# A hybrid encoder block: where tiles lie modulo 256 bytes, and which engine scales the first half of each mid norm

## The chip, the core and the metric

The kernel runs on one core of a Trainium2 chip. It computes in float32, its large products as fp32r, and is one launch. The metric is the device time of that launch in microseconds. TensorE (PE in the profile) multiplies; VectorE (DVE), ScalarE (ACT) and GpSimd (POOL) do the rest; SyncE (SP) issues every DMA. A tile in SBUF has 128 partitions, and where it lies is given by its first byte within a partition.

## The reference

One layer of a bidirectional encoder on 1024 tokens of width 1024. Each sub-layer is normed before and after, and added to the residual:

```python
h = _rms_norm(x, g_mix_pre[l])
proj = h @ w_in[l]
...
mix = jnp.concatenate([attn_o, dn_o], axis=-1) @ w_out[l]
x = x + _rms_norm(mix, g_mix_post[l])
c = _memory_cross_attention(_rms_norm(x, g_cross_pre[l]), _rms_norm(mem, g_mem[l]),
                            w_cq[l], w_ckv[l], w_co[l])
x = x + _rms_norm(c, g_cross_post[l])
f = _swiglu(_rms_norm(x, g_ffn_pre[l]), w_gate_up[l], w_down[l])
x = x + _rms_norm(f, g_ffn_post[l])
```

attn_o is a windowed attention, dn_o a gated delta rule that is scanned in both directions, and the cross attention reads 256 memory tokens.

## The kernel before

**Products.** Every float32 operand of a large product is split into two fp32r parts, hi (a rounding on ScalarE, L102) and lo (the rest, on VectorE or GpSimd, L103, or L106 with a scale). A product is three matmuls: hi by hi, hi by lo, lo by hi. `load_w` fetches a block of weights (`wraw`) and makes `whi` and `wlo` of it, two blocks in flight.

**Stages, in order of time.** The input projections with the convolutions and chunk preparations of the delta rule (matmuls `pg` on L261; `wabr` on L315 is a short extra projection); the scans (`psc`) between windows of attention and the memory's keys and values (`pck`, `pcv`); `mid_gemm` for the output projection (`pmg`, L1016), once for each half of the tokens; the cross attention (`pcq`, `pcs`, `pco`); `mid_gemm` again; the gate and up projections in seven products of sums and differences of quarters (`pA`, `pB`, `pD`, `pE`, L1191); the down projection (`pdA`, `pdD`, `pdX`, L1381 and L1474). A scheduler orders the instructions of each engine; `ORDER_1` to `ORDER_3` set the order in which the early parts are issued to it.

**A mid norm.** After its eight blocks of weights, `mid_gemm` does for each of four tiles of 128 tokens: GpSimd makes the first rstd (L1028, L1029), VectorE scales z and adds the residual (L1030), ScalarE squares z and sums it (L1033), GpSimd makes the second rstd from that (L161, L162), and ScalarE scales z by it into `xr` (L1036). `turn_norm` or `turned_k` then turns `xr` on TensorE. A call with `hf` 0 is the first half of the tokens, and its turning comes while the second half's product already runs.

**Rows of the profile.** A matmul reads out<-streamed operand, weights: in `pA<-s,whi` the activations `s` stream past the weights `whi`; in `pmg<-whi,b` the weights' block streams past the activations `b`. Names are tags: `b` is any tile of opB (activations at the left), `s` the first operand of opA (at the right), `x` the one of opC, `s0h` to `s3l` sums of weights.

**Where tiles lie.** Pools grow from both ends of the SBUF. The left end holds `cst` first (ident 512 bytes, mhalf 64, phalf 64, cols 512, from byte 16512), then `wp` (the weights' blocks) and most others; the right end holds `off` (a tile of 32 bytes, which only takes room) and then those pools that are opened with `side="right"`. In the built program, modulo 256:

| tiles | end | before | after |
|---|---|---|---|
| wraw, whi, wlo, opB (b), opC (x), opB3, dhl, t4h, t4l, bhi, blo, ph, vhl, qs, khi, kr, vr, mT, U | left | 0 | 192 |
| cph, cpl | left | 128 | 192 |
| hhi, hlo, opA (s), s0h to s3l, sr, pz, kv of the scan, S, mraw, gt | right | 192 | 192 |
| wabr, xt, z and xr of the second mid_gemm | right | 64 | 64 |
| z and xr of the first mid_gemm | left | 0 | 192 |
| ident (what turns a tile) | left | 128 | 128 |

Of the kernel before, what the change touches and what calls it, by code (L numbers as in the profile page):

```python
# [10 lines left out]
F32 = mybir.dt.float32  # L11
F32R = mybir.dt.float32r
I32 = mybir.dt.int32
AF = mybir.ActivationFunctionType
ALU = mybir.AluOpType
# [4 lines left out]
P = 128  # L20
# [55 lines left out]
def tile_hybrid_block(  # L76
# [6 lines left out]
    nc = tc.nc  # L83
# [24 lines left out]
    def pool(name, bufs, **kw):  # L108
        return tc.tile_pool(name=name, bufs=bufs, reuse_waits="tile", **kw)

    cst = ctx.enter_context(pool("cst", 1))
# [6 lines left out]
    def load_w(src, k, n, eng=None, after=None):  # L118

        with tc.high_priority(AHEAD):  # L120
            raw = wp.tile([P, k, n], F32, tag="wraw", name="wraw")
            with ExitStack() as order_:
                if after:
                    order_.enter_context(tc.issue_after(after.ins))
                nc.sync.dma_start(raw, src.rearrange("(k p) n -> p k n", p=P))
            hi = wp.tile([P, k, n], F32R, tag="whi", name="whi")
            lo = wp.tile([P, k, n], F32R, tag="wlo", name="wlo")
            split(hi, lo, raw, eng=eng)
        return hi, lo
# [2 lines left out]
    ident = cst.tile([P, P], F32, name="ident")  # L132
    mhalf = cst.tile([P, 16], F32, name="mhalf")
    nc.gpsimd.memset(mhalf, -0.5)
    phalf = cst.tile([P, 16], F32, name="phalf")
    nc.gpsimd.memset(phalf, 0.5)
    cols = cst.tile([P, P], F32, name="cols")
    p12 = ExitStack()
# [19 lines left out]
    def rstd_of(rs, ss, n, eps):  # L158

        w = ss.shape[-1]  # L160
        nc.gpsimd.tensor_scalar(rs, ss, n, eps, ALU.mult, ALU.add)  # L161
        nc.gpsimd.tensor_tensor(rs, rs, mhalf[:, :w], ALU.pow)  # L162
# [836 lines left out]
    def mid_gemm(tz, act, w, gp, res, dst, hf, between=None):  # L999


        zs = [tz.tile([P, D], F32, tag="z", name="z", bufs=4) for _ in range(4)]
        sss = [tz.tile([P, 2], F32, tag="zss", name="zss", bufs=8) for _ in range(4)]
        for ch in range(2):
            cs = slice(ch * 512, (ch + 1) * 512)
            if ch and between:
                between()
            pp = [pg.tile([P, 512], F32, tag="pg", name="pmg") for _ in range(4)]
            for kp in range(4):
                whi, wlo = load_w(w[kp * 256:(kp + 1) * 256, cs], 2, 512)  # L1010
                for t in range(4):
                    tt = slice(t * P, (t + 1) * P)
                    for kk in range(2):
                        k = 2 * kp + kk
                        for i, (w_, a) in enumerate(((whi, 0), (whi, 1), (wlo, 0))):
                            nc.tensor.matmul(pp[t], act[a][:, k, tt], w_[:, kk, :], start=(k == 0 and i == 0),  # L1016
                                             stop=(k == KT - 1 and i == 2))
            for t in range(4):
                nc.scalar.activation(zs[t][:, cs], pp[t], AF.Square, accum_out=sss[t][:, ch:ch + 1])
                nc.vector.tensor_tensor(zs[t][:, cs], pp[t], gp[:, cs], ALU.mult)  # L1020
        xn = []
        for t in range(4):
            tok = slice(hf * HALF + t * P, hf * HALF + (t + 1) * P)
            z = zs[t]
            xr = tz.tile([P, D], F32, tag="xr", name="xr", bufs=XR)
            nc.sync.dma_start(xr, res[tok, :])
            rs = tz.tile([P, 1], F32, tag="prs", name="prs", bufs=4)
            nc.gpsimd.tensor_scalar(rs, sss[t][:, 1:2], sss[t][:, 0:1], D * EPS, ALU.add, ALU.add)  # L1028
            nc.gpsimd.tensor_tensor(rs, rs, mhalf[:, 0:1], ALU.pow)  # L1029
            nc.vector.scalar_tensor_tensor(z, z, rs, xr, ALU.mult, ALU.add)  # L1030
            nc.sync.dma_start(dst[tok, :], z)
            s2 = tz.tile([P, 1], F32, tag="ps2", name="ps2", bufs=4)
            nc.scalar.activation(xr, z, AF.Square, accum_out=s2)  # L1033
            r2 = tz.tile([P, 1], F32, tag="pr2", name="pr2", bufs=4)
            rstd_of(r2, s2, 1.0 / D, EPS)
            nc.scalar.activation(xr, z, AF.Identity, scale=r2)  # L1036
            xn.append(xr)
        return xn

# [11 lines left out]
    for hf in range(2):  # L1051
        for kp in range(4):
# [4 lines left out]
            split(mxT[hf][0][:, k2, :], mxT[hf][1][:, k2, :], raw[:, k2, :])  # L1057
    LR.close()
    xn0 = mid_gemm(tz, mxT[0], w_out, gp, x, d_x1, 0)
    h2T = [[opB.tile([P, KT, HALF], F32R, tag=b1, name=b1), opB_first[2]]]  # L1060
    xn1 = mid_gemm(tz, mxT[1], w_out, gp, x, d_x1, 1, between=lambda: turn_norm(xn0, "cross", *h2T[0], pin=True))
    h2T.append(operand(opA, "s0"))
    turn_norm(xn1, "cross", *h2T[1])
# [8 lines left out]

    L2 = ExitStack()
    tx = L2.enter_context(pool("tx", 2))

    def cross_q(hf):
        q = operand(opB, ("s1", "s2")[hf])
        for ct in range(KT):
            whi, wlo = load_w(w_cq[:, ct * P:(ct + 1) * P], KT, P, nc.gpsimd)
            pp = [pg.tile([P, 512], F32, tag="pg", name="pcq")]  # L1080
            gemm_b(whi, wlo, h2T[hf:hf + 1], pp)
            split(q[0][:, ct, :], q[1][:, ct, :], pp[0])
        return q
# [60 lines left out]
    def blocks(t):  # L1144
        return t[:, 0:HK], t[:, HK:KT]

    xn = mid_gemm(tz, q0, w_co, gp, d_x1, d_x2, 0)
    x1h, x1l = operand(opA, "s0")
    X11, X21 = (x1h[:, 0:HK], x1l[:, 0:HK]), (x1h[:, HK:KT], x1l[:, HK:KT])
# [252 lines left out]
    def residual(t, after=None):  # L1402
        xr = tp_.tile([P, D], F32, tag="xrf", name="xrf")
        with tc.issue_after((after or late).ins):
            nc.sync.dma_start(xr, d_x2[t * P:(t + 1) * P, :])
        return xr
# [57 lines left out]
    for t in range(4):  # L1464
# [14 lines left out]
        xr = residual(r)  # L1479
# [40 lines left out]
```

## Time and profile before

| | before |
|---|---|
| median of 3 runs | 1562.68 us (1558.62 to 1563.87) |
| the profiled execution, its own time | 1562.86 us |
| its span | 1561.1 us |
| mean granted TensorE clock | 0.99 |
| HBM read, written | 173.65 MB, 69.50 MB |
| matmuls, weight loads | 7451, 7451 |

Busy time of an engine is a union of its instructions; a matmul's recorded length overlaps its successor's, so the distance of two starts, not the length, tells how fast TensorE goes. Idle time behind a group of instructions is put down to what ended it. The lines themselves stand where they are used.

### The profile page before, as it was taken

How to read it: one execution, taken by the hardware profiler on the slowest of the kernel's cores; microseconds unless marked ns; L12 is line 12 of the kernel's file. 1: busy time of each engine (PE TensorE's matmuls, PEld its weight loads, DVE VectorE, ACT ScalarE, POOL GpSimd, SP SyncE). 2: the span in 40 equal slices, each digit the busy share in tenths (PEclk: the TensorE clock that was granted, in tenths of full speed). 3: DMA queues.
4: the chain of work that ended last, by engine and by line, in shares of the span. 5: the costliest groups of instructions: out<-in, count | busy, mean ns of one | idle time of the engine just before them, and what ended most of it. 6: DMA issues, size and time to landing. Idle time of an engine off the chain costs nothing.

```text
span 1561.1 us, 20936 instructions
## 1 busy us (share of the span) xinstructions
PE 1504.1 (96%) x7451; PEld 1252.7 (80%) x7451; DVE 1052.3 (67%) x1742; ACT 726.5 (47%) x1388; POOL 308.8 (20%) x305
## 2 busy tenths in 40 slices
PE   6999999988999999999999999999999999999998
PEld 5888787877899777888888877888888888888786
DVE  6777888767998855434346377776867554696665
ACT  6665552346557765453336574322222222454532
POOL 2000110000004102153102221443433333000021
PEclk9999999999999999999999999999999999999999
DMA  6244446868987674354213254333433334753354
GB/s 208 70 130 121 130 146 159 219 176 273 336 268 251 199 268 149 116 169 147 68 54 135 97 190 139 115 125 119 157 119 109 101 102 138 286 195 102 108 174 164
DMA packets 267367, 247.17 MB, mean 158 GB/s; under 512 B 39016, under 2 KB 204797, under 8 KB 267261
## 3 DMA queue, kind: packets, MB, share of 16 engines
q1 hardware_dynamic: 267261, 245.82, 49.6%
q8 instruction: 59, 0.97, 0.2%
q14 instruction: 47, 0.39, 0.1%
HBM read 173.65 MB, written 69.50 MB: 156 GB/s over the span
## 4 chain that ended last, share of the span: by engine, by line
PE 78%; DVE 7%; DMA 6%; ACT 3%; issue 2%; SPq 2%; POOL 1%; DVEq 0%; POOLq 0%; ACTq 0%
PE pg L261 13%; PE pmg L1016 10%; PE pD L1191 8%; PE pE L1191 8%; PE pA L1191 6%; PE pcq L261 6%; PE pdX L1381 6%; PE pdA L1381 4%; PE pB L1191 4%; PE pdD L1381 2%; PE psc L785 2%; PE pcs L1097 1%; PE pco L1123 1%; DVE wlo L103 1%; PE pdX L1474 1%
## 5 line engine op out<-in xcount | busy, mean ns | idle before, releaser
L102 ACT CAST whi<-wraw 128x1024 fp32r<-128x1024 f32 x108 | 113.1, 1048 | 170.6 <-PE pg L261 38.4
L103 DVE TENSOR_TENSOR wlo<-wraw,whi 128x1024 fp32r<-128x1024 f32 x78 | 95.5, 1225 | 87.4 <-ACT whi L102 83.3
L261 PE MATMUL pg<-hhi,whi 128*128 128x512 f32 x352 | 142.1, 405 | 1.5 <-DVE rop L730 1.5
L261 PE MATMUL pg<-hhi,wlo 128*128 128x512 f32 x352 | 141.0, 401 | 0.0
L261 PE MATMUL pg<-hlo,whi 128*128 128x512 f32 x352 | 141.0, 401 | 0.0
L1016 PE MATMUL pmg<-whi,b 128*128 128x512 f32 x384 | 120.0, 399 | 2.6 <-ACT whi L102 2.2
L1191 PE MATMUL pA<-s,whi 128*128 128x512 f32 x352 | 111.4, 397 | 1.2 <-ACT m L1208 1.2
L103 POOL TENSOR_TENSOR wlo<-wraw,whi 128x1024 fp32r<-128x1024 f32 x30 | 73.9, 2464 | 147.0 <-ACT whi L102 138.8
L1016 PEld LDWEIGHTS pmg<-whi,b 128*128 128x128 f32 x384 | 72.2, 191 | 18.2 <-ACT whi L102 2.6
L261 PEld LDWEIGHTS pg<-hhi,whi 128*128 128x128 f32 x352 | 67.0, 191 | 16.7 <-DVE rop L730 2.0
L261 PEld LDWEIGHTS pg<-hlo,whi 128*128 128x128 f32 x352 | 67.0, 190 | 14.8
L1191 PEld LDWEIGHTS pA<-s,whi 128*128 128x128 f32 x352 | 65.2, 187 | 16.8 <-ACT m L1208 1.9
L261 PEld LDWEIGHTS pg<-hhi,wlo 128*128 128x128 f32 x352 | 66.7, 190 | 14.7
L1381 PE MATMUL pdX<-dhl,whi 128*128 128x512 f32 x264 | 76.1, 390 | 1.5 <-DVE zv L1436 0.8
L1016 PE MATMUL pmg<-wlo,b 128*128 128x512 f32 x192 | 71.5, 392 | 0.0
L1191 PE MATMUL pA<-s,wlo 128*128 128x512 f32 x176 | 69.7, 397 | 1.1 <-DVE wlo L103 1.1
L102 ACT CAST whi<-araw 128x1024 fp32r<-128x1024 f32 (+1 forms) x36 | 35.3, 982 | 71.3 <-PE pdX L1381 27.6
L1268 POOL TENSOR_TENSOR act<-act,up 128x512 f32<-128x512 f32 x33 | 50.1, 1519 | 91.1 <-DVE up L1267 54.3
L103 DVE TENSOR_TENSOR wlo<-araw,whi 128x1024 fp32r<-128x1024 f32 (+1 forms) x36 | 40.8, 1133 | 40.2 <-ACT whi L102 40.2
L286 DVE SCALAR_TENSOR_TENSOR acc<-cp,cols,acc 128x1024 f32<-128x1024 f32 x48 | 61.4, 1281 | 1.5 <-ACT acc L284 0.9
L1381 PEld LDWEIGHTS pdX<-dhl,whi 128*128 128x128 f32 x264 | 49.3, 188 | 12.8 <-issue 1.1
L1241 DVE TENSOR_TENSOR sr<-sr,wraw 128x512 f32<-128x512 f32 x22 | 38.1, 1732 | 29.1 <-POOL sr L1240 29.1
(408 smaller groups left out, 3971.9 us busy)
## 6 DMA issues: line engine op xcount, KB each, us to landing
wraw<-in_w_gate_up_dram SPq DMA_DIRECT2D x52, 512.0 KB, 3.9
kv<-d_kv SPq DMA_DIRECT2D x32, 512.0 KB, 6.7
wraw<-in_w_in_dram SPq DMA_DIRECT2D x22, 512.0 KB, 4.6
b<-in_w_down_dram SPq DMA_DIRECT2D x20, 512.0 KB, 6.8
araw<-d_as SPq DMA_DIRECT2D x20, 512.0 KB, 3.6
pz<-d_pz SPq DMA_DIRECT2D x32, 256.0 KB, 6.5
wraw<-in_w_ckv_dram SPq DMA_DIRECT2D x16, 512.0 KB, 7.1
wraw<-in_w_out_dram SPq DMA_DIRECT2D x16, 512.0 KB, 4.2
```

The lines of the kernel that those rows point to most:

```text
L102: nc.scalar.copy(hi, src)
L103: (eng or nc.vector).tensor_tensor(lo, src, f32(hi), ALU.subtract)
L261: nc.tensor.matmul(p_, w[:, k, :], ah[a][:, k, :], start=(k == 0 and i == 0), stop=(k == nk - 1 and i == 2))
L286: nc.vector.scalar_tensor_tensor(acc, cp[:, t:t + S], taps[t], acc, ALU.mult, ALU.add)
L785: nc.tensor.matmul(out[:, d, h, :], lt[:, d, h, :], rt[:, d, h, :], start=True, stop=True)
L1016: nc.tensor.matmul(pp[t], act[a][:, k, tt], w_[:, kk, :], start=(k == 0 and i == 0), stop=(k == KT - 1 and i == 2))
L1097: nc.tensor.matmul(pp[:, t2_, :], q[a][:, ct, tt], kr_[b_][:, ct, :], start=(j == 0 and i == 0), stop=(j == 1 and i == 2))
L1123: nc.tensor.matmul(po, vr_[a][:, kt, cs], pts[kt][b_], start=(kt == 0 and i == 0), stop=(kt == 1 and i == 2))
L1191: nc.tensor.matmul(out_, w[a][:, k, :], xx[b_][:, k, :], start=(start and k == 0 and i == 0), stop=(k == HK - 1 and i == 2), skip_group_ch ...
L1241: nc.vector.tensor_tensor(s[1], s[0], a_[:, 0:HK], ALU.subtract)
L1268: nc.gpsimd.tensor_tensor(o_, o_, up, ALU.mult)
L1381: nc.tensor.matmul(banks[t], a[:, k - k0, tt], w, start=(first and k == 0 and i == 0), stop=(k == NB - 1 and i == 2), skip_group_check=not ...
```

## The change

It has three parts. `phalf` is made 64 columns wide and used as before through its first 16, so everything behind it at the left moves by 192 bytes. In the cross attention's pool `tx`, the two tags `cph` and `cpl` get a tile each at the head of the pool, ahead of the small `cmx` and `csum`; these early tiles are never used. In `mid_gemm`, the last scaling goes to VectorE where `hf` is 0 and stays on ScalarE where it is 1.

```diff
-    phalf = cst.tile([P, 16], F32, name="phalf")
+    phalf = cst.tile([P, 64], F32, name="phalf")[:, 0:16]
     nc.gpsimd.memset(phalf, 0.5)
...
             rstd_of(r2, s2, 1.0 / D, EPS)
-            nc.scalar.activation(xr, z, AF.Identity, scale=r2)
+            if hf:
+                nc.scalar.activation(xr, z, AF.Identity, scale=r2)
+            else:
+                nc.vector.tensor_scalar(xr, z, r2, None, ALU.mult)
             xn.append(xr)
...
     tx = L2.enter_context(pool("tx", 2))
+    for n in ("cph", "cpl"):
+        tx.tile([P, 512], F32R, tag=n, name=n, bufs=2)
```

The order of instructions hardly changes. On ScalarE, in the first mid norm (the first half of the output projection's result), the place is this; `ps` and `pr` are the sum of squares and the second rstd of a tile:

```order
 L1033 ACTIVATE xr,ps_6328<-z 128x1024
 L1033 ACTIVATE xr,ps_6341<-z 128x1024
-L1036 ACTIVATE xr<-z,pr_6330 128x1024
-L1036 ACTIVATE xr<-z,pr_6343 128x1024
 L1033 ACTIVATE xr,ps_6354<-z 128x1024
 L1033 ACTIVATE xr,ps_6367<-z 128x1024
-L1036 ACTIVATE xr<-z,pr_6356 128x1024
-L1036 ACTIVATE xr<-z,pr_6369 128x1024
 L102 CAST whi<-wraw 128x1024 x3
 L1019 ACTIVATE z,zss<-pmg 128x512 x3
```

The four scalings leave ScalarE, and the rounding of the next three weight blocks follows the four squares directly. On VectorE at the same place the first tile's scaling now stands between the third and the fourth residual sum, and the other three behind it, ahead of the next three `wlo`:

```order
 L1020 TENSOR_TENSOR z<-pmg,gpost 128x512
-L1030 SCALAR_TENSOR_TENSOR z<-z,prs,xr 128x1024 x2
+L1030 SCALAR_TENSOR_TENSOR z<-z,prs,xr 128x1024
+L1039 TENSOR_SCALAR xr<-z,pr_6330 128x1024
+L1030 SCALAR_TENSOR_TENSOR z<-z,prs,xr 128x1024
+L1039 TENSOR_SCALAR xr<-z,pr_6343 128x1024
+L1039 TENSOR_SCALAR xr<-z,pr_6356 128x1024
+L1039 TENSOR_SCALAR xr<-z,pr_6369 128x1024
 L103 TENSOR_TENSOR wlo<-wraw,whi 128x1024 x3
```

What moved is the same four scalings; each waits for GpSimd's rstd, and the lo parts of three weight blocks stand behind them. In the second mid norm (the first half of the cross attention's result) VectorE's queue after the change is this, in the midst of the other half's attention (`pco`, `pcs`):

```order
L1030 SCALAR_TENSOR_TENSOR z<-z,prs,xr 128x1024
L1039 TENSOR_SCALAR xr<-z,pr_8284 128x1024
L1030 SCALAR_TENSOR_TENSOR z<-z,prs,xr 128x1024
L103 TENSOR_TENSOR wlo<-wraw,whi 128x1024
L1020 TENSOR_TENSOR z<-pmg,gpost 128x512
L1039 TENSOR_SCALAR xr<-z,pr_8297 128x1024
L103 TENSOR_TENSOR b_7409<-pco,b_7408 128x512
L1030 SCALAR_TENSOR_TENSOR z<-z,prs,xr 128x1024
L103 TENSOR_TENSOR b_7409<-pco,b_7408 128x512
L1039 TENSOR_SCALAR xr<-z,pr_8310 128x1024
L1039 TENSOR_SCALAR xr<-z,pr_8323 128x1024
L1104 TENSOR_REDUCE cmx<-pcs 128x2
```

Before, the same rows without the four of L1039 stood there, the two `b` rows together behind the last L1030. On TensorE only a few matmuls of `pmg` in that second norm's stage change places; GpSimd and SyncE keep their order.

## Prediction

> **What bounds the kernel now.** I read the page's busy shares first, then the chain that ended last.
>
> ```profile
> PE 1504.1 (96%) x7451; PEld 1252.7 (80%) x7451; DVE 1052.3 (67%) x1742; ACT 726.5 (47%) x1388; POOL 308.8 (20%) x305
> ...
> PE 78%; DVE 7%; DMA 6%; ACT 3%; issue 2%; SPq 2%; POOL 1%; DVEq 0%; POOLq 0%; ACTq 0%
> ```
>
> TensorE is occupied 96% of the span and is 78% of the chain. So the time is mostly a number of matmuls times the distance from one to the next. Since a busy matmul is not a matmul at its peak, I read that distance next, stage by stage. The view by stretches of time shows where TensorE is dense.
>
> ```profile
> 20.00:360.00 340.00, 329.97 (x1678) 274.43 (x1678) 263.95 (x497) 166.51 (x325) 20.63 (x44) 0.98 0.53 147
> 360.00:560.00 200.00, 185.70 (x1313) 169.77 (x1312) 166.73 (x442) 132.56 (x345) 28.16 (x43) 0.97 0.81 264
> ...
> 660.00:900.00 240.00, 237.42 (x1185) 197.74 (x1184) 108.56 (x162) 115.83 (x225) 65.48 (x56) 1.00 0.35 116
> 900.00:1340.00 440.00, 434.86 (x1891) 351.71 (x1891) 302.31 (x374) 155.67 (x250) 155.39 (x106) 1.00 0.40 131
> 1340.00:1561.00 221.00, 211.85 (x930) 173.68 (x928) 151.51 (x210) 92.36 (x150) 18.82 (x18) 0.99 0.50 169
> ```
>
> The first pair of numbers after the length is TensorE's busy time and its matmuls; the last three are the granted clock, the DMA share and GB/s. From 660 to 1340 us TensorE hardly rests, and the clock is the same there (1.00) as in the last stage (0.99). Now the distance. In the timeline of TensorE the first column is a start and the last a count (a row of x2 holds two), so I count the matmuls between two rows.
>
> ```profile
> 1349.62 0.39 PE L1381 MATMUL pdA<-dhl,wlo 128*128 128x512 f32 x1
> ...
> 1350.98 0.39 PE L1381 MATMUL pdA<-dhl,wlo 128*128 128x512 f32 x1
> ...
> 1053.05 0.39 PE L1191 MATMUL pA<-s,wlo 128*128 128x512 f32 x1
> ...
> 1054.45 0.39 PE L1191 MATMUL pA<-s,wlo 128*128 128x512 f32 x1
> ...
> 110.05 0.39 PE L261 MATMUL pg<-hhi,wlo 128*128 128x512 f32 x1
> ...
> 110.75 0.39 PE L261 MATMUL pg<-hhi,wlo 128*128 128x512 f32 x1
> ...
> 1055.85 0.40 PE L1191 MATMUL pB<-b,s1l 128*128 128x512 f32 x1
> ...
> 1056.55 0.40 PE L1191 MATMUL pB<-b,s1l 128*128 128x512 f32 x1
> ...
> 1048.26 0.39 PE L1191 MATMUL pD<-x,s3l 128*128 128x512 f32 x1
> ...
> 1048.95 0.39 PE L1191 MATMUL pD<-x,s3l 128*128 128x512 f32 x1
> ```
>
> All are fp32r matmuls of 512 columns without a wait. In the down projection (pdA) six take 1.36 us, 0.2267 each. In pA six take 1.40, 0.2333 each; in pg and pB three take 0.70, the same; in pD three take 0.69, 0.230. Against the table of places above: pdA has both operands at 0 modulo 256; pA and pg stream from 192 with weights at 0; pB and pD stream from 0 with weights at 192. So unequal places go with 3.3 to 6.6 ns more. Is it the far end of the SBUF, rather than the difference? Two loops say no.
>
> ```profile
> 751.19 0.39 PE L1123 MATMUL pco<-cpl,vr 128*128 128x512 f32 x1
> ...
> 751.88 0.40 PE L1123 MATMUL pco<-cpl,vr 128*128 128x512 f32 x1
> ...
> 48.24 0.39 PE L315 MATMUL pg<-hhi,wabr 128*128 128x512 f32 x1
> ...
> 50.10 0.40 PE L315 MATMUL pg<-hhi,wabr 128*128 128x512 f32 x1
> ```
>
> pco has both operands at the left, at 128 and 0: three in 0.69, 0.230. The wabr loop has both at the right, at 192 and 64: eight in 1.86, 0.2325. Both are slow, so a common end doesn't help. And pB and pD, alike in their places, are spaced differently (0.233 and 0.230): a toll on one operand would be constant, while two streams that get in each other's way depend on how they fall into step. That is my reason to believe in the difference.
>
> **The change part by part.** *Places.* By the program, 3120 of the 512-column matmuls go from unequal to equal: 1776 that stream from 192 with weights at 0 (pg 1056, pcq 192, pA 528), 1056 that stream from 0 with weights at 192 (pB, pD, and pE's first half), 192 in pmg and 96 in pco. Only wabr's 32 stay unequal. The first 1776 gain 0.2333 - 0.2267 = 6.6 ns each: 11.7 us. For the 1056 the rows above bound it by 3.3 and 6.6 ns, 3.5 to 7.0 us; the mean lengths tell which is nearer.
>
> ```profile
> L1381 PE MATMUL pdA<-dhl,whi 128*128 128x512 f32 x176 | 52.1, 389 | 0.0
> ...
> L1191 PE MATMUL pA<-s,whi 128*128 128x512 f32 x352 | 111.4, 397 | 1.2 <-ACT m L1208 1.2
> ...
> L1191 PE MATMUL pD<-x,s3h 128*128 128x512 f32 x176 | 55.3, 396 | 1.8 <-DVE u L1308 1.8
> ...
> L1191 PE MATMUL pE<-b,s2l 128*128 128x512 f32 x88 | 34.4, 391 | 0.0
> ...
> L1016 PE MATMUL pmg<-whi,s 128*128 128x512 f32 x128 | 38.2, 393 | 1.5 <-ACT whi L102 1.5
> ```
>
> The second number behind the bar is the mean length. The eight groups of the 1056 run from 391 (s2l) to 396 (s3h), between pdA's 389 and pA's 397, so I take 4 ns: 4.2 us. pmg's 393 is halfway, 3.3 ns, and pco's spacing gives 3.3: together 288 x 3.3 = 0.9 us. The sum is 16.8 us, with bounds 16.1 and 20.6 (6.6 ns for all 3120).
>
> What of it lies on the path? Of the 16.8, 7.0 are pg's (1056 x 6.6 ns) and lie before 360 us, where TensorE idles 10 of 340 us and VectorE is busy 264 of them: some waits there end by VectorE or a DMA and will only grow. I take off a quarter, 1.8 us; the ends are nothing and all 7.0. From 660 to 1340 us TensorE idles 7.7 of 680 us, and I take off nothing. Left: 15.0 us. From 360 to 560 and from 1340 on no pair changes between equal and unequal.
>
> No pair above has both operands at 192. That 192 with 192 runs like 0 with 0 is the inference on which the forecast stands.
>
> The Trainium skill, on "SBUF — State Buffer", section "Who interferes with whom", gives TensorE two independent read ports, for streamed operand and weights, and says that it never waits on anyone; by it, moving both would change nothing. The 0.2267 and 0.2333 of this trace don't fit that, unless another cause separates the loops.
>
> *The scaling.* Four ACTIVATEs on L1036 per first-half norm, eight in all, leave ScalarE and come back as VectorE's TENSOR_SCALAR. Before, in the first norm, they stand ahead of the weights' rounding (L102) that TensorE waits for:
>
> ```profile
> 617.45 1.16 ACT L1036 ACTIVATE xr<-z,pr 128x1024 f32<-128x1024 f32 x1 [1.78 <-POOL pr L162]
> ...
> 618.92 1.15 ACT L1036 ACTIVATE xr<-z,pr 128x1024 f32<-128x1024 f32 x1 [0.32 <-POOL pr L162]
> ...
> 622.05 2.18 ACT L1036 ACTIVATE xr<-z,pr 128x1024 f32<-128x1024 f32 x2
> ...
> 624.14 1.98 ACT L102 CAST whi<-wraw 128x1024 fp32r<-128x1024 f32 x2
> 625.20 2.36 DVE L103 TENSOR_TENSOR wlo<-wraw,whi 128x1024 fp32r<-128x1024 f32 x2 [7.00 <-ACT whi L102]
> ...
> 625.22 3.66 PE L1016 MATMUL pmg<-whi,b 128*128 128x512 f32 x8 [2.18 <-ACT whi L102]
> ```
>
> TensorE stands still 2.18 us. The time on VectorE is known from another norm with the same shape:
>
> ```profile
> L894 DVE TENSOR_SCALAR mt<-mt,mrs x2: 746/750/753, 379.9 to 381.3; 128x1024 f32<-128x1024 f32 x2
> ```
>
> Four take 3.0 us, and VectorE idles 7.0 us there ahead of wlo, which is their cover. The four wait for POOL's rstd and stand ahead of wlo x3, so wlo waits too. My reckoning: ScalarE ends its fourth L1033 near 620.5 (the two late ones no longer wait behind 2.3 us of L1036), the cast ends near 621.6, VectorE ends its fourth scaling near 622.4 and the first wlo near 623.6. TensorE ran dry at about 623.0 and takes eight whi matmuls (1.8 us) before a wlo. So the 2.2 us go. Without the cover the four cost at most 3.0 us, which leaves a loss of 0.8; I take the gain. In the second norm (830 to 847 us) no idle of TensorE hangs on L1036; the same four lie beside the attention of the other half. I cost it at nothing, cover gone 3.0.
>
> *The rest.* The early cph and cpl tiles issue nothing: they only move those two tags to the pool's front, and pco is in the sum. The wider phalf's memset still covers 16 columns.
>
> *Moved DMA ends.* Tiles at the left now begin at 192 instead of 0. Two loads of one shape show what that may cost:
>
> ```profile
> mraw<-d_mix SPq DMA_DIRECT2D x4, 512.0 KB, 7.9
> b<-d_mix SPq DMA_DIRECT2D x4, 512.0 KB, 9.2
> ...
> d_u<-U SPq DMA_DIRECT2D x8, 256.0 KB, 2.8
> d_gate<-gt SPq DMA_DIRECT2D x8, 256.0 KB, 3.0
> ```
>
> mraw lies at 192, b at 0, and mraw is the quicker one. Of two stores, U (at 0) takes 2.8 and gt (at 192) 3.0, 7% more. DMA is 6% of the chain, 94 us, so the bounds are 0 and 94 x 7% = 6.6 us; I take 0, the loads being most of it. The Trainium skill, "DMA: Bandwidth & Descriptors", section "How a descriptor splits into AXI transactions", speaks against the change here: a descriptor that doesn't start at a multiple of 256 bytes costs extra beats (25 instead of 18 in its example of 576 bytes). By that rule the transfers would lengthen; mraw's 7.9 beside b's 9.2 doesn't show it.
>
> **The sum.** 15.0 + 2.2 = 17.2 us off. The profiled execution took 1562.9 us (span 1561.1), and the median of the runs is 1562.7, so nothing has to be carried over: 1562.9 - 17.2 = 1545.7.
>
> **The rivals.**
> - *A toll on any start that is not 0.* Then 192 with 192 is as slow as 192 with 0. For it: each slow loop above has an operand away from 0, and none has two equal ones elsewhere. Against it: pB and pD differ though placed alike, and the wabr loop, with two operands off 0, pays no double toll. Price: the equal pairs of today (pmg's b 576, pdA, pdX and pdD 924 with the last ones, pcq's b 192, pE's second half 264, pcv and pow 184) are 2140; 2140 x 6.6 ns = 14.1 us, and the 1056 and 288 rise to the full toll, 2.6 x 1056 + 3.3 x 288 = 3.7 us. Less 2.2 from the norm: 1562.9 + 15.6 = 1578.5. It decides as soon as pdA's spacing is over 0.2267. Chance 0.11.
> - *The spacing belongs to the loops, not to the places.* Only the norm's 2.2 us come: 1560.7. For it: the unequal loops are also those with other banks and neighbours. Against: pco and wabr. Chance 0.08. The Trainium skill's rule on the ports, above, would give this one.
> - *Moved DMA ends cost.* 6.6 us of the gain are given back: 1552.3. Chance 0.05.
> - *My forecast*, 1545.7: chance 0.76. Its own ends are 1562.9 - 20.6 - 2.2 = 1540.1, and, with all of pg's 7.0 us swallowed and the norm's loss of 0.8 in both norms' place, 1562.9 - 9.1 + 0.8 = 1554.6; with 3.0 us lost in the second norm, 1557.6.
>
> **How the numbers follow.** The range 1540 to 1557.5 takes in the forecast's ends and the DMA rival, 0.81 together. A measurement of this kernel can tell about 0.3%, 4.7 us, from no change. Faster by more than that are the forecast and the DMA rival, 0.81; within it is the loops' rival, 0.08; slower is the toll, 0.11.
>
> **What would show it.** Right: pA's and pg's six in 1.36 us and pdA's still in 1.36; the wabr loop unchanged at 0.2325; no idle of TensorE ahead of the whi matmuls after the first norm; TENSOR_SCALARs near 0.75 us. Wrong: pdA at 1.40 (the toll), pA still at 1.40 (the loops), longer landings of wraw (DMA), wlo late behind the scaling and TensorE idle on VectorE there. If every spacing falls but the span falls by less than 12 us, the waits before 360 us have grown.

## The result

The changed kernel takes 1550.87 us (median of 6 runs, 1548.51 to 1555.78), beside 1561.86 us before (6 runs, 1558.62 to 1563.87). The ratio is 0.993, with an interval of 0.9911 to 0.9949. It is faster by some 11 us, inside the range that was given, and 5 us short of the forecast of 1545.7. The profiled execution took 1555.78 us (span 1554.1). It is the slowest of the six runs, so positions and spacings are read from it, and the size of the effect from the medians.

The page's busy shares and its chain, after:

```profile
PE 1497.3 (96%) x7451; PEld 1258.1 (81%) x7451; DVE 1055.9 (68%) x1750; ACT 719.6 (46%) x1380; POOL 308.3 (20%) x305
...
PE 80%; DVE 6%; DMA 6%; ACT 3%; issue 2%; SPq 2%; POOL 0%; DVEq 0%; POOLq 0%; ACTq 0%
```

The picture is that of before: TensorE is occupied, and little else is on the chain. VectorE has its eight instructions more and ScalarE eight fewer. What changed is the distance of the matmuls. TensorE's timeline after, the same five kinds as before (first column the start, last the count):

```profile
1342.27 0.39 PE L1386 MATMUL pdA<-dhl,wlo 128*128 128x512 f32 x1
...
1342.95 0.39 PE L1386 MATMUL pdA<-dhl,wlo 128*128 128x512 f32 x1
...
1053.27 0.39 PE L1196 MATMUL pA<-s,wlo 128*128 128x512 f32 x1
...
1053.95 0.39 PE L1196 MATMUL pA<-s,wlo 128*128 128x512 f32 x1
...
107.65 0.39 PE L261 MATMUL pg<-hhi,wlo 128*128 128x512 f32 x1
...
108.33 0.39 PE L261 MATMUL pg<-hhi,wlo 128*128 128x512 f32 x1
...
1054.63 0.39 PE L1196 MATMUL pB<-b,s1l 128*128 128x512 f32 x1
...
1055.31 0.39 PE L1196 MATMUL pB<-b,s1l 128*128 128x512 f32 x1
...
1047.15 0.39 PE L1196 MATMUL pD<-x,s3l 128*128 128x512 f32 x1
...
1047.83 0.39 PE L1196 MATMUL pD<-x,s3l 128*128 128x512 f32 x1
...
48.00 0.39 PE L315 MATMUL pg<-hhi,wabr 128*128 128x512 f32 x1
...
49.86 0.39 PE L315 MATMUL pg<-hhi,wabr 128*128 128x512 f32 x1
```

In each of the first five pairs the second row is the third matmul behind the first, and it starts 0.68 us later: 0.2267 in each of these loops, with both operands now at 192. The wabr loop, still unequal, takes 1.86 us for eight as before, 0.2325. Over all matmuls of a kind, the mean distances of consecutive starts (those up to 0.262 us, so without waits) give the size:

| matmuls | before, ns | after, ns | gain, us |
|---|---|---|---|
| pg, 1056 | 233.2 | 227.9 | 5.6 |
| pA, 528 | 233.3 | 227.1 | 3.3 |
| pB, pD, pE's first half, 1056, by operand | 228.3 to 232.3 | 226.4 to 226.9 | 4.4 |
| pcq that streams s, 192 | 233.3 | 227.9 | 1.0 |
| pmg that streams whi, wlo past s, 192, and pco, 96 | 229.1, 232.3 | 227.2, 227.4 | 0.8 |
| pdA, with 264 matmuls (equal before and after) | 226.7 | 226.7 | 0.0 |

Together 15.1 us. The means hide something that the rows show. Here are two places of one loop in the kernel before, pE's first half, which streams from 0 with weights at 192:

```profile
1006.22 0.40 PE L1191 MATMUL pE<-b,s2l 128*128 128x512 f32 x1
...
1006.92 0.40 PE L1191 MATMUL pE<-b,s2l 128*128 128x512 f32 x1
...
1039.36 0.39 PE L1191 MATMUL pE<-b,s2l 128*128 128x512 f32 x1
...
1040.05 0.39 PE L1191 MATMUL pE<-b,s2l 128*128 128x512 f32 x1
```

Three matmuls take 0.70 us at the one place and 0.69 at the other, in the same loop and with the same places in memory. Counted in ns from one lo row to the next of the same loop, a group of three took 680 in all 68 groups of pdA, 697 to 703 in 131 of 133 groups of pA, and in pB, pD and pE's first half either 686 or 687 (148 of 261) or 700 (113). So these loops had three speeds before the change, and only equal places had the fastest. After it, 63 of pB's 64 groups and all 66 of pE's first half took 680, but only 117 of pA's 132 and 205 of pg's 268; the rest of those are slower, which is why pg's mean stays at 227.9. pE's second half had equal places before too, yet only 37 of its 66 groups took 680 then, and the slow ones stood at the start of a block; all but one took 680 after.

The norm went as forecast as well. TensorE's waits from 612 to 640 us were this one row before, and there is none after:

```profile
PE pmg L1016 <- ACT whi L102: 2.2, 1, 2.2
```

The window of 625 to 629 us, before and then after, shows in addition the granted clock (the third number from the end):

```profile
625.00:629.00 4.00, 3.78 (x10) 3.02 (x11) 2.36 (x2) 1.12 (x2) 0.00 (x0) 0.57 0.27 91
```

```profile
625.00:629.00 4.00, 4.00 (x19) 3.08 (x17) 2.65 (x4) 2.11 (x2) 1.85 (x3) 1.00 0.21 85
```

Ten matmuls before and nineteen after. The trace lists the granted clock as stretches, called records here: behind the wait of 2.2 us the clock fell to half for one record of 3.41 us, and that went with the wait. So each term shows in the trace, yet the sum came short. A ledger tells where. It compares the start of the same matmul in both traces; negative is ahead of before:

| matmul of before at | in the changed kernel, us |
|---|---|
| 300 us | -4.5 |
| 392 us | -0.1 |
| 407 us | +4.5 |
| 620 us | +4.3 |
| 632 us | +0.4 |
| 1340 us | -6.7 |
| 1500 us | -6.6 |

The lead from pg is lost between 300 and 407 us, and more than the lead. From 620 us on the gains come and stay.

### The profile page after: what moved, and what is told of

It reads as the page before. It is cut to its first block, busy times and chain, and to the rows that moved or that the text cites. A ratio compares the mean times of both kernels' runs of the same rounds, so it can differ in the third digit from the quotient of the medians.

```text
span 1554.1 us, 20931 instructions
## 1 busy us (share of the span) xinstructions
PE 1497.3 (96%) x7451; PEld 1258.1 (81%) x7451; DVE 1055.9 (68%) x1750; ACT 719.6 (46%) x1380; POOL 308.3 (20%) x305
## 4 chain that ended last, share of the span: by engine, by line
PE 80%; DVE 6%; DMA 6%; ACT 3%; issue 2%; SPq 2%; POOL 0%; DVEq 0%; POOLq 0%; ACTq 0%
PE pg L261 13%; PE pmg L1016 10%; PE pD L1196 8%; PE pE L1196 8%; PE pA L1196 6%; PE pcq L261 6%; PE pdX L1386 6%; PE pdA L1386 4%; PE pB L1196 4%; PE psc L785 2%; PE pdX L1479 2%; PE pdD L1386 2%; DMA wraw<-in_w_ckv_dram 2%; PE pcs L1102 1%; PE pco L1128 1%
```

## The experiments

**First: which part does what, and is the loss a matter of the clock?** In this profile of the changed kernel the records of half clock, without the one at the very end, add up to 47.8 us, against 27.3 before. Theory A: half clock took the missing 5 us. Theory B: the waits from 300 to 375 us give pg's lead back at any clock.

The changed kernel once more, unedited.

> The changed kernel once more, nothing edited, for a second profile. Theory A (the missing 5 us of the forecast went to stretches in which TensorE's clock was granted at half: 47.8 us of them in the first profile of after, 27.3 before): a profile with about 27 us of half clock has a span near 1546, and the lead of 3.5 us that TensorE had at the windows of attention (364 us) is still there at 390 us. Theory B (the waits between 300 and 375 us give the lead back whatever the clock): the span stays at 1549 or more at any clock, and the lead at 390 us is 0.

Measured: 1549.98 us (5 runs, 1547.08 to 1551.34), ratio 0.9924 (0.9909 to 0.9939). Half clock adds up to 27.3 us, as before the change, and yet the span of 1548.8 is 12.3 us shorter, not 17; the lead was 4.4 us at 300 and 0.6 at 392. A alone doesn't explain it: B expected a span of 1549 or more and no lead, and comes nearer.

Places alone: the change without the scaling.

```diff
-            if hf:
-                nc.scalar.activation(xr, z, AF.Identity, scale=r2)
-            else:
-                nc.vector.tensor_scalar(xr, z, r2, None, ALU.mult)
+            nc.scalar.activation(xr, z, AF.Identity, scale=r2)
```

> The places of after, with all scaling left on ScalarE as before. The forecast's sum gives 15.0 us under before, 1547; by the ledger of after's first profile the norm was worth 3.9 us and the places about 7 to 8, 1554. Spacing of pA, pB, pD and pg 0.2267 as in after, TensorE still idle for about 2.2 us ahead of the whi matmuls of the first norm.

Measured: 1555.43 us (5 runs, 1553.14 to 1556.3), ratio 0.9956 (0.9942 to 0.9971): some 5 us off, where the term was 15.0 and the ledger had led to 7 or 8.

Scaling alone: the kernel before with the four lines that were taken out above.

> The places of before, with the scaling of the first halves on VectorE. The forecast gives 2.2 us under before (1559.7). If the 2.2 us of idle also cost the 3.4 us of half clock that followed it at 625 us in before, the gain is 3.9 us (1558). A loss of 0.8 would mean that wlo comes late. Spacing of pA 0.2333 as before.

Measured: 1558.2 us (12 runs, 1554.54 to 1560.43), ratio 0.998 (0.997 to 0.999), 2.6 us. In its trace the lead grows by 3.9 us between 620 and 632 us, 2.2 of it the wait and 1.7 the half clock behind it. The two belong together: all five traces with the scaling on ScalarE have a record of half clock that starts between 619 and 626 us, and none of the nine traces with it on VectorE has one.

Equal at 0: the kernel before with the right end moved down by 192 bytes, in place of the left end up by 192. pco and wabr stay unequal, ScalarE scales.

```diff
-    nc.gpsimd.memset(off.tile([P, 8], F32, name="off"), 0.0)
+    nc.gpsimd.memset(off.tile([P, 56], F32, name="off")[:, 0:8], 0.0)
```

> Before, with the right end moved down by 192 bytes instead of the left end up: both ends at 0 modulo 256, cph and cpl still at 128, scaling on ScalarE. If the difference of the places counts: the same as places alone but for pco's 96 matmuls, within 1 us of it, pA and pB at 0.2267. If it counts that the left end was moved (its DMA ends, its starts), time as before.

Measured: 1550.32 us (6 runs, 1549.41 to 1554.1), ratio 0.9931 (0.9917 to 0.9945). In its TensorE timeline the loops go as fast as with both operands at 192:

```profile
1051.74 0.39 PE L1191 MATMUL pA<-s,wlo 128*128 128x512 f32 x1
1052.42 0.39 PE L1191 MATMUL pB<-b,s1l 128*128 128x512 f32 x1
1053.10 0.39 PE L1191 MATMUL pB<-b,s1l 128*128 128x512 f32 x1
```

These are rows of lo weights; two matmuls of hi stand between each pair, and the three take 0.68 us. So neither 192 nor the far end is what counts for the distance, but that the two are equal. What was not foreseen is that this kernel, without the scaling, is as fast as the whole change, and 5 us faster than places alone at 192.

**Second: does pg's gain arrive at all, does equality also rule the down projection, and is 0 better than 192?** Theory S: the stretch from 296 to 384 us swallows pg's gain. Theory C: it reaches the end.

pg apart: in the changed kernel only hhi and hlo lie 64 bytes further, at 0.

```diff
+    hx.tile([P, 16], F32, name="gap0")
     hT = []
...
         hT.append((hi, lo))
         dump(f"hT{hf}", (hi, lo))
+    hx.tile([P, 48], F32, name="gap1")
```

> The changed kernel, but with hhi and hlo 64 bytes further, at 0 modulo 256, so that the 1056 matmuls of pg (all before 360 us) are unequal again (0 with 192) and everything else stays equal. Spacing of pg back from 0.228 to 0.230 to 0.233 us in both theories, which is 2.5 to 5.3 us more on TensorE before 300 us. Theory S (pg's gain is swallowed by the waits between 296 and 384 us, whose ends are set by SyncE's queue, the round trip of d_q and VectorE): the time stays that of the changed kernel, 1550 +- 1.5 us, and TensorE is no more than 1.5 us later at 392 us than in the changed kernel. Theory C (pg's gain is carried, and what is missing went into stretches of half clock): 1553 to 1556 us.

Measured: 1550.94 us (6 runs, 1546.85 to 1553.48). This did not tell the theories apart: streaming from 0 past weights at 192, pg went at 229.7 ns, between 229.3 and 230.3 by operand, so that only some 2 us were undone, which is within the spread of the runs. It is 2.8 us above the changed kernel beside it, which follows, and 1.0 above all 17 runs of that kernel.

The changed kernel once more, beside it:

> The changed kernel beside the others on the same chip: 1550 +- 1.5 us in every theory; its trace is one more sample of how much of the lead at 296 us (4.4 us in the two so far) is left at 384 and 560 us. Theory S expects 0 to 1.5 us at 384 us whatever the clock records show; Theory C expects the lost part to equal the half-clock stretches that this run has more than the kernel before.

Measured: 1548.15 us (6 runs, 1546.67 to 1552.34). Span 1545.0, and a lead of 2.8 us left at 392 us, of 3.3 at 300. That is against both A and B as they were put: the lead isn't always lost, and half clock (23.9 us here) was no greater than before.

The down projection apart: 64 bytes at the head of the pool that holds dhl, the streamed blocks of w_down, so that the 924 matmuls of pdA, pdD and pdX stream from 0 while the operand at the right in their rows (whi, wlo) stays at 192.

```diff
+    kz.tile([P, 16], F32, tag="gap", name="gap")
```

> The changed kernel, but with a gap of 64 bytes at the head of the down projection's pool, so that its 924 matmuls (pdA, pdD, pdX) stream from 0 with weights at 192; they were equal before and after. Theory of equality: spacing of pdA from 0.2267 to 0.230 to 0.233 us, 3 to 6 us more, and nothing swallows it, since TensorE has no long waits there: 1553 to 1556 us. Rival (spacing belongs to the loops of pg, pA to pE): pdA stays at 0.2267 and the time at 1550 us.

Measured: 1552.24 us (6 runs, 1551.46 to 1552.8), 4.1 above the changed kernel beside it and 2.3 above the 1549.98 of all its 17 runs. The timeline:

```profile
1347.67 0.39 PE L1387 MATMUL pdA<-dhl,wlo 128*128 128x512 f32 x1
...
1349.73 0.39 PE L1387 MATMUL pdA<-dhl,wlo 128*128 128x512 f32 x1
```

Nine matmuls in 2.06 us are 0.2289, against 0.2267; the means go from 226.7 to 229.0 for pdA and from 227.0 to 230.5 for those of pdX that stream dhl. A loop that had been fast becomes slow by being moved: spacing doesn't belong to the loops. The time stayed under the 1553 to 1556 us that were expected, as pdA and pdD rose to the middle one of the three speeds, 686 to 689 ns in all of their groups.

The right end at 0 with all the rest of the change:

```diff
-    nc.gpsimd.memset(off.tile([P, 8], F32, name="off"), 0.0)
+    nc.gpsimd.memset(off.tile([P, 56], F32, name="off")[:, 0:8], 0.0)
...
-    phalf = cst.tile([P, 64], F32, name="phalf")[:, 0:16]
+    phalf = cst.tile([P, 16], F32, name="phalf")
```

> All three parts of the change, but equality made by moving the right end to 0 (off of 224 bytes) in place of the left end to 192; cph and cpl at 0 as well, wabr's 32 at 128 with 0. If the places of the left end's DMAs (192 instead of 0) cost something: 1545 to 1548 us, 2 to 5 us below the changed kernel. If only equality counts: 1550 +- 1.5 us, like the changed kernel.

Measured: 1545.96 us (5 runs, 1543.79 to 1547.16), ratio 0.9891 (0.9875 to 0.9907), the fastest kernel so far.

**Third: both questions once more, with cleaner pairs.** Theory D: the places of the left end's DMAs cost something at 192.

The last kernel with hhi and hlo alone back at 192, exactly the pair of before (192 with 0):

```diff
+    hx.tile([P, 48], F32, name="gap0")
     hT = []
...
         dump(f"hT{hf}", (hi, lo))
+    hx.tile([P, 16], F32, name="gap1")
```

> The kernel with the right end at 0 and the scaling on VectorE, but hhi and hlo alone back at 192, so that pg's 1056 matmuls are the pair of before (192 with 0) and all else stays equal. pg's spacing 0.2333 us, 5.0 to 5.6 us more on TensorE before 340 us. Theory S (the stretch from 296 to 556 us swallows pg's gain): at most 1.5 us slower than the same kernel with pg equal, which is run beside it (1546 us so far). Theory C (pg's gain reaches the end): 4 to 6 us slower, 1550 to 1552 us.

And the same without that edit:

> The right end at 0 and the scaling on VectorE, again, for comparison with the run that has pg apart: 1546 +- 1.5 us in every theory.

Measured: 1548.16 us (6 runs, 1546.26 to 1554.77) against 1545.08 (5 runs, 1541.69 to 1547.15). pg is back at 233.2 ns, 5.5 us more on TensorE; 3.1 of them reach the end by the medians (2.6 against all ten runs of the other kernel). Resampling the runs gives 95% intervals of 0.4 to 8.6 and 0.7 to 6.8 for these two, so they are rough. In the two traces the lead over before at 300 us is 0.4 and 5.6 us, at 392 us 0.4 and 3.2. So the answer lies between S and C: about half is swallowed by the medians, and neither theory came out as it was put.

Places alone at 192 and the right end at 0, both without the scaling, again side by side:

> The places of the change alone, again (left end at 192, scaling on ScalarE). Theory D (the left end's DMA ends at 192 cost something): 3 to 6 us slower than the run beside it that has the right end at 0, 1554 to 1556 us. If the first difference was chance: within 1.5 us of it, near 1552 us. Weights' loads that land 0.1 us later (4.0 where the kernel before has 3.9 for gate_up) speak for D.

> The kernel before with the right end moved to 0, again (left end at 0, scaling on ScalarE). Theory D: 1550 +- 1.5 us. If the first difference was chance: within 1.5 us of the run with the left end at 192, near 1552 us.

Measured: 1553.61 us (6 runs, 1552.29 to 1557.13) and 1549.83 us (6 runs, 1545.99 to 1551.86): 3.8 us, no run in common, after 5.1 us the first time. With the scaling, side by side, it was 2.2 us (1548.15 and 1545.96). Three comparisons have one sign: both ends at 192 are slower than both at 0, as D expected. Over all runs it is 3.6 us without the scaling (1553.66 in 11 runs, 1550.04 in 12; interval 2.3 to 6.3) and 4.5 us with it (1549.98 in 17 runs, 1545.52 in 10; interval 2.5 to 6.8).

Does 192 cost the DMAs anything? The queue's row has its packets, their MB and the time they took, as a share of 16 engines over the span. First the kernel before (span 1561.1 us), then places alone, where the left end has moved (1551.5), then the right end at 0, where only the right end has moved (1552.4):

```profile
q1 hardware_dynamic: 267261, 245.82, 49.6%
```

```profile
q1 hardware_dynamic: 267261, 245.82, 51.1%
```

```profile
q1 hardware_dynamic: 267261, 245.82, 49.9%
```

Share times span is 774, 793 and 775 us of each engine's time, for the same packets. In all seven traces with the left end at 0 it is 771 to 775, wherever the right end lies, and in all seven with the left end at 192 it is 785 to 793. So the transfers do take some 2% longer, and it is the left end's move that does it.

Where does that cost time? The DMA issues of the changed kernel, and behind them those of the kernel with the right end at 0 and the scaling on VectorE (the last number is the median from issue to landing, in us):

```profile
wraw<-in_w_gate_up_dram SPq DMA_DIRECT2D x52, 512.0 KB, 4.0
...
wraw<-in_w_cq_dram SPq DMA_DIRECT2D x16, 512.0 KB, 3.7
...
xr<-d_x SPq DMA_DIRECT2D x8, 512.0 KB, 9.1
```

```profile
wraw<-in_w_gate_up_dram SPq DMA_DIRECT2D x52, 512.0 KB, 3.8
...
wraw<-in_w_cq_dram SPq DMA_DIRECT2D x16, 512.0 KB, 3.5
...
xr<-d_x SPq DMA_DIRECT2D x8, 512.0 KB, 8.5
```

In the seven traces with the left end at 192 the gate_up blocks land in 4.0 to 4.1 us, those of w_cq in 3.6 to 3.7 and xr in 8.8 to 9.1; in the seven with it at 0, before among them, in 3.8 to 3.9, 3.4 to 3.6 and 8.5 to 8.7. These are the groups that separate. The xr of this row did not move with the change (it is that of the second norm, at the right), so its own place isn't what delays it. The blocks of w_in, w_out, w_ckv and w_co moved like those of gate_up, and their medians overlap (w_out 3.9 to 4.4 with the left end at 192, 3.9 to 4.3 at 0). Busy times of VectorE, ScalarE and GpSimd differ by some 1% at most between kernels with the same scaling, and the shorter matmuls keep their distances (pcs 119.3 to 119.4 ns in all 14 traces, psc of S 104.5 to 104.9).

The ledger tells the stage. Between 392 and 620 us TensorE gains 1.3 to 3.8 us on the kernel before in the five traces with both ends at 0, and loses 0.0 to 4.4 in the seven with both at 192 (scaling alone, with the left end at 0 and the right one at 192, gains 1.4); the part of the lead that is lost between 300 and 392 us overlaps (2.4 to 5.0 us in the four of the five that have a lead from pg, 0.5 to 4.4 in the seven). One place where a landing holds TensorE is the memory's keys: the rounding of a block of w_ckv on ScalarE, and the matmul that needs it. ScalarE's row and TensorE's of the changed kernel, and then of the other kernel:

```profile
399.77 1.04 ACT L102 CAST whi<-wraw 128x1024 fp32r<-128x1024 f32 x1 [3.43 <-DMA wraw<-in_w_ckv_dram]
...
400.87 0.80 PE L916 MATMUL pck<-mT,whi 128*128 128x256 f32 x2 [2.03 <-ACT whi L102]
```

```profile
393.65 1.04 ACT L102 CAST whi<-wraw 128x1024 fp32r<-128x1024 f32 x1 [1.14 <-DMA wraw<-in_w_ckv_dram]
...
395.04 0.48 PE L916 MATMUL pck<-mT,whi 128*128 128x256 f32 x2
```

In the bracket is the idle time ahead. ScalarE waits 3.43 us for the landing and then TensorE 2.03 for ScalarE; with both ends at 0 it is 1.14 and nothing. TensorE waits 0.5 to 2.0 us here in all seven traces with both ends at 192, and at most 0.2 in all five with both ends at 0; the two with the left end at 0 and the right one at 192, before among them, wait 0.6 and 0.7. In this trace half clock came with the wait. The window around it, first of the changed kernel and then of the other:

```profile
396.00:407.00 11.00, 7.95 (x39) 7.17 (x40) 6.82 (x22) 5.88 (x14) 0.20 (x1) 0.69 0.95 283
```

```profile
396.00:407.00 11.00, 11.00 (x89) 10.71 (x89) 10.66 (x31) 5.42 (x13) 0.00 (x0) 1.00 0.99 350
```

39 matmuls at a clock of 0.69 against 89 at 1.00, in a stretch where the DMA engines are busy all the time (share 0.95 and 0.99). Four of the seven traces with both ends at 192 have a record of half clock that starts between 397 and 400 us, and none of the other seven has. That the longer transfers are the cause of the 4 us is how I read these rows: their lengthening by the left end's move is shown, and so is the stage of the loss, but no run lengthened the transfers and left the matmuls' places alone, and the waits at the keys, 0.5 to 2.0 us, are only a part of the 4 us.

## Why the prediction was right, and where it was short

**Spacing: right in mechanism, a little large in size.** Equal places give 0.2267 in each loop that is shown, at 192 and at 0; unequal ones are slower, even in a loop that was fast. The rival with a toll on any start away from 0 fell (pdA kept 0.2267), and so did the one with spacing belonging to the loops (the down projection became slow). The term was 16.8 us and measured 15.1. The 1056 of pB, pD and pE were sized well (4.2, measured 4.4). The overestimate is pg's 7.0, measured 5.6: its equal pairs go at 227.9 ns, not at pdA's 226.7. One reason that the prediction gave for the difference of places was read from too few rows: pB at 0.233 and pD at 0.230 are each one pair of rows. By the means pB goes at 231.0 and pD's part that streams x at 231.9, and both loops have groups of 687 and of 700 ns. What holds of that argument is that a single loop, with its places fixed, has two speeds, which a constant toll on one operand doesn't give. Why there are just three speeds stays open.

**What is swallowed before 360 us: somewhat larger.** A quarter of 7.0, 1.8 us, was taken off. The pair of runs with pg apart and equal says 2.4 to 2.9 of 5.5, within the rough intervals above.

**Scaling: right, and too small.** The wait of 2.2 us went, and TENSOR_SCALAR took 0.754 us as forecast. The half clock behind the wait had been overlooked, 1.7 us more in the trace. The medians give 2.6 us alone, and 3.7 and 4.5 with places equal at 192 and at 0. In the second norm nothing showed.

**Moved DMA ends: the term that was wrong.** The prediction took 0 between bounds of 0 and 6.6 us, on the ground that mraw at 192 landed sooner than b at 0 (7.9 beside 9.2). That compared two tensors at different moments. The same packets took 785 to 793 us of each engine's time with the left end at 192 and 771 to 775 with it at 0, and the runs put 3.6 to 4.5 us between both ends at 192 and both at 0; that the one causes the other is my reading, as said above. The rival of moved DMA ends, 1552.3 us at a chance of 0.05, was nearer to the result than the forecast. The Trainium skill, "DMA: Bandwidth & Descriptors", section "How a descriptor splits into AXI transactions", was right in sign here, with 793 beside 774 us in the rows above; the effect is a small part of its example's 25 beats for 18. The Trainium skill, "SBUF — State Buffer", section "Who interferes with whom", by which TensorE's two read ports are independent, is contradicted by these runs for the two streams of fp32r matmuls: 680 ns for three with equal places, 687 or 700 without.

**How much of it was luck.** The forecast came within 5 us of the result partly because two errors have opposite signs: the scaling gave 1.5 to 2.3 us more than its 2.2 once places were equal, and the moved ends cost 3.6 to 4.5 where nothing had been put down.

The sum with measured terms, by medians: spacing 15.1, less 2.4 to 2.9 swallowed, plus 3.7 to 4.5 for the scaling, is 15.9 to 17.2 us. The kernel with both ends at 0 has all of these terms and leaves the left end where it was; it gained 16.0 and 17.4 us beside the kernel before in its two groups of runs. Less 3.6 to 4.5 for the ends at 192, 11.4 to 13.6 are left for the change as it was made; its three groups of runs show 11.0, 10.8 and 13.8. Only the 16.0 and 17.4 test the sum; the last step doesn't, for the 3.6 to 4.5 are the difference of these two kernels. What stays open is how the losses between 296 and 560 us divide: waits and half clock trade places from run to run there (the lead at 392 us of the same changed kernel was 0.1, 0.6 and 2.8 us).

## What to carry to other kernels

Place the streamed operand and the weights of fp32r matmuls so that their starts are equal modulo 256 bytes (modulo 512, to be safe, as the last section says), and choose 0 as the common place if DMAs also write there: here that is 1545.5 us against 1550.0. Judge a DMA's place only by the same transfers in two kernels, and by the time of all packets, never by two transfers of one kernel. Price a wait of TensorE with the half clock that may follow it. And don't count a gain in full that lies ahead of a stretch of DMAs and waits: here about half of it came through, with a wide interval.

## What the runs showed of the hardware

- The distance of fp32r matmuls of 512 columns depends on where the streamed operand and the weights start within 256 bytes: by the means of their loops 226.4 to 228.8 ns where the places are equal (at 0 or at 192; pcv, below, aside), 228.3 to 233.6 where they are not. The ranges touch, so a loop is to be compared with itself.
- Long loops have three speeds: 680 ns for three matmuls with equal places, 686 or 687, and 700. A loop that streams from 0 past weights at 192 can have either of the slower two, block by block.
- Order matters: streaming from 192 past weights at 0, pA, pg and pcq stayed near 700 (pg 233.2 ns each); streaming from 0 past weights at 192, pg took 229.7 ns, and 686 or 687 for most of its groups of three.
- In the built program nearly all equal pairs are also equal modulo 512. Of those that lie 256 apart there, only pcv (96 matmuls) is a loop long enough to judge; its median is 227 ns in the kernel before and its mean 229.1. So 256 rests on that loop.
- The same DMA packets took some 2% longer with the SBUF's left end at 192 modulo 256 than at 0: 785 to 793 against 771 to 775 us of each engine's time.
- The granted clock fell to half behind a single wait of TensorE of 2.2 us (at 625 us in the kernel before), and in less dense stretches behind idle times of 1.8 and 1.3 us (at 260 and 526 us), for records of 3.41 us or a multiple of it. How many of them a run has differs from run to run of one kernel (47.8, 27.3 and 23.9 us ahead of the end in three profiles of the changed kernel).
